# Zero-padded keys by head for the first dilation group's scores in an encoder trunk

## The chip, the cores and the metric

The kernel runs on one core of a Trainium2 chip. The metric is the device time of one execution in microseconds; lower is better. Engines are named as in the profile: PE is TensorE's matmuls, PEld its weight loads, DVE is VectorE, ACT is ScalarE, POOL is GpSimd, SP is the engine that issues the DMAs.

## The reference

A trunk of four residual layers over one sequence of 256 tokens and 1024 channels. Each layer has a token mixer and a SwiGLU channel mixer, each between two RMS norms. Layers 0 and 3 mix by retention, layer 1 by a convolution module, layer 2 by dilated attention. The change is in layer 2. There, 16 heads of 64 channels have three groups of queries, keys and values, one for each dilation (1, 4, 16); the outputs of the three groups are merged by their softmax denominators:

```python
def _dilated_attention_mixer(h, w_in, w_out):
    proj = (h @ w_in).reshape(B, S, N_ATTN_GROUPS, 3, ATTN_HEADS, ATTN_HEAD_DIM)
    ...
    for g, (window, dil) in enumerate(DILATION_GROUPS):   # (128, 1), (512, 4), (2048, 16)
        q = prope(proj[:, :, g, 0])
        k = prope(proj[:, :, g, 1])
        v = proj[:, :, g, 2]
        o, l = _dilated_band_attention(q, k, v, dil, window // (2 * dil))
        outs.append(o)
        lses.append(l)
    wts = jax.nn.softmax(jnp.stack(lses, 0), axis=0)
    o = jnp.sum(wts[..., None] * jnp.stack(outs, 0), axis=0).astype(h.dtype)
    return o.reshape(B, S, ATTN_HEADS * ATTN_HEAD_DIM) @ w_out
```

Merging by the denominators is the same as one softmax over the keys of all three groups side by side, and the kernel does it so.

## The kernel before

The tokens are two tiles of 128 (t = 0, 1), reordered so that tokens of the same residue modulo 4 lie together. Every float32 operand of a product is kept as two parts, a high part in the format that TensorE takes and the low rest; a product is then three matmuls (high x high, high x low, low x high). `split` (line 49) makes the parts: line 50 copies the high part on ScalarE, line 51 subtracts it from the source on VectorE. Weights come through `load_w` by DMA into one of seven raw buffers and are split in the same way into one of ten pairs of buffers `wh`, `wl`.

The attention layer (`attention`) loops over eight pairs of heads. For a pair it projects queries, keys and values (`roped` and `vproj`, both through `proj`, whose matmuls are line 181: 24 of 384 columns for one tile of tokens), turns queries and keys with identity matmuls (`flip3`, L693) into a PSUM bank with channels in the rows, and splits them. `kflip` (L706) does this for the keys: the bank holds 128 rows by three blocks of 128 columns. Block 0 holds the keys of dilation 1, head 0 in rows 0 to 63 and head 1 in rows 64 to 127; one split of 128x128 puts it into `kh`, `kl` (tags `akh`, `akl`). Blocks 1 and 2 hold, for head 0 and head 1, the two other dilations in the two halves of the rows; they go by two splits of 64x256 into `kbh`, `kbl`, whose other places were set to zero once, at lines 670 and 671.

`softmax(t, h, st)` (L724) makes the scores of one tile of queries and one head into one PSUM bank: the first 256 columns are dilation 1, three matmuls of line 729 that contract the 64 rows of head h; the last 256 columns are the two other dilations, three matmuls of line 731 that contract all 128 rows, where the zeros in `kbh`, `kbl` keep the dilations apart. Then VectorE adds the mask and takes the row's extreme (L736), ScalarE takes the exponential (L746), and VectorE normalises (L747, L748). For a pair it is called four times, (t, h) = (0,0), (0,1), (1,0), (1,1).

The probabilities are turned (`flip`, L757) and multiplied with the values (`values`, L772: 12 matmuls of 256 columns) inside the next pair's projections. So TensorE's order for a pair is: the scores of the pair before, query projection, two flips, key projection, and so on up to the value projection of tile 1, after which its own scores follow. The second `kflip` of a pair stands ahead of the value projection of tile 1 (inside it for the first pair). The framework lists the instructions of each engine by priority and readiness in a model of its own, so weight casts for the next pair stand between the small steps on ScalarE and VectorE, and the order on an engine is fixed when the kernel is built. Accesses to one PSUM bank are ordered among engines by semaphores.

Of the kernel before, what the change touches and what calls it, by code (L numbers as in the profile page):

```python
# [8 lines left out]
F32 = mybir.dt.float32  # L9
F32R = mybir.dt.float32r  # L10
# [4 lines left out]
P = 128  # L15
D = 1024
# [4 lines left out]
PAIRS = 8  # L21
# [16 lines left out]
def tile_trunk(ctx: ExitStack, tc: tile.TileContext, a):  # L38
    nc = tc.nc
# [9 lines left out]
    def split(h, l, src):  # L49
        ia = nc.scalar.copy(h, src)  # L50
        iv = nc.vector.tensor_sub(l, src, h.bitcast(F32))  # L51
        return ia, iv
# [23 lines left out]
        with tc.issue_after(cast[0].ins), tc.issue_after(cast[1].ins):  # L76
            yield

# [1 line left out]
    xs = [const.tile([P, D], F32, tag=f"x{t}", name=f"x{t}") for t in range(2)]  # L80
    grow = work.tile([1, D], F32, tag="gain", name="grow", bufs=2)
    nc.sync.dma_start(grow, a["norm_w"][0:1, :])
# [120 lines left out]
                    stop=(last and i == 2),  # L203
                )

# [1 line left out]
    def retention_decay(j, pool):  # L207
        tmp = pool
        dist = work.tile([P, 2, 512], F32, tag="fg", name="dist", bufs=1)
# [19 lines left out]
            dts.append(dt)  # L229
        return dts  # L230

# [1 line left out]
    def retention(j, gload, decay, finish, pool, first):  # L233
        dts = []
        rope = pool.tile([P, 2, 2, P], F32, tag="rope", name="rope", bufs=1)
# [276 lines left out]
    def conv(j, finish, pool, prefetch):  # L512
# [9 lines left out]
        cvp = pool.tile([P, KB, 256], F32, tag="cvp", name="cvp", bufs=1)  # L522

        def perm(v):
            # natural token 4 u + r, read as (r, u)
            return v.rearrange("p (u r) -> p r u", r=4)

        def glu(t, c, ws, mid=None):
# [80 lines left out]
        for t in range(2):  # L609
# [15 lines left out]
            h = const.tile([P, KB, P], F32R, tag=f"xTh{t}", name=f"yh{t}")  # L625
            l = const.tile([P, KB, P], F32R, tag=f"xTl{t}", name=f"yl{t}")
            for hh in range(2):
                tp = bank("aux")
# [34 lines left out]
    def attention(j, finish, pool):  # L663
# [5 lines left out]
        kbl = pool.tile([P, 2, 2, 256], F32R, tag="kbl", name="kbl", bufs=1)  # L669
        nc.vector.memset(kbh.bitcast(F32), 0.0)  # L670
        nc.vector.memset(kbl.bitcast(F32), 0.0)
        oh = pool.tile([P, PAIRS, 256], F32R, tag="oh", name="oh", bufs=1)
        ol = pool.tile([P, PAIRS, 256], F32R, tag="ol", name="ol", bufs=1)

# [21 lines left out]
        def ts_(t):  # L696
            return slice(t * P, (t + 1) * P)
# [7 lines left out]

        def kflip(t, st, r):  # L706
            tp = flip3(r)
            if t == 0:
                st["kh"] = pool.tile([P, 256], F32R, tag="akh", name="akh", bufs=1)
                st["kl"] = pool.tile([P, 256], F32R, tag="akl", name="akl", bufs=1)  # L710
            split(st["kh"][:, ts_(t)], st["kl"][:, ts_(t)], tp[:, 0:P])
            tv = tp[:, P : 3 * P].rearrange("p (h d) -> p h d", h=2)
            for rows, cols in ((slice(0, 64), slice(0, P)), (slice(64, P), slice(P, 256))):
                split(kbh[rows, :, t, cols], kbl[rows, :, t, cols], tv[rows])
# [7 lines left out]
            split_scaled(st["vh"][:, t, :], st["vl"][:, t, :], b[:, 0:384], rsx[t])  # L722

        def softmax(t, h, st):  # L724
            qh, ql, kh, kl = st["qh"], st["ql"], st["kh"], st["kl"]
            rows = slice(h * 64, h * 64 + 64)
            b = bank("acc")
            for n, (x, y) in enumerate(((qh, kh), (qh, kl), (ql, kh))):
                nc.tensor.matmul(b[:, 0:256], lhsT=x[rows, 0, ts_(t)], rhs=y[rows, :], start=(n == 0), stop=(n == 2))  # L729
            for n, (x, y) in enumerate(((qh, kbh), (qh, kbl), (ql, kbh))):  # L730
                nc.tensor.matmul(  # L731
                    b[:, 256:512], lhsT=x[:, 1 + h, ts_(t)], rhs=y[:, h, t, :], start=(n == 0), stop=(n == 2)
                )
            pe = pool.tile([P, 512], F32, tag="ape", name="ape", bufs=APE)
            sc = work.tile([P, 4], F32, tag="asc", name="asc", bufs=4)
            nc.vector.tensor_tensor_reduce(  # L736
                out=pe,
                in0=b,
                in1=mask[:, t, :],
                op0=ALU.add,  # L740
                op1=ALU.min,
                scale=-0.125,
                scalar=3e38,
                accum_out=sc[:, 0:1],
            )
            nc.scalar.activation(pe, pe, AF.Exp, scale=-1.0, bias=sc[:, 0:1], accum_out=sc[:, 1:2])  # L746
            nc.vector.reciprocal(sc[:, 2:3], sc[:, 1:2])  # L747
            nc.vector.tensor_scalar_mul(pe, pe, sc[:, 2:3])  # L748
            return pe
# [38 lines left out]
        for pr in range(PAIRS):  # L788
            st = {"wq": w3(pr, 0)}
# [53 lines left out]
        outp(1, range(4, KB))  # L843
        finish(1, acc[1])

# [1 line left out]
    pre_norm(0, gain0, late=True)  # L847

    for i in range(DEPTH):
# [3 lines left out]
        def finish(t, f):  # L853
            post_norm(t, f, gains[0])
            pre_norm(t, gains[1])
# [27 lines left out]
            ffn(i, finish_ffn, pool)  # L883


# [1 line left out]
def _layout(inputs):  # L887
    import numpy as np

    f32 = np.float32  # L890
    pos = np.arange(256)
    tok = 4 * (pos % 64) + pos // 64
    c = {}
    c["x"] = inputs["x"].reshape(256, D)[tok].reshape(2, P, D)
    c["ident"] = np.eye(P, dtype=f32)
    c["norm_w"] = inputs["norm_w"].reshape(4 * DEPTH, D)
    c["log1m"] = inputs["ret_log1m_decay"].reshape(-1, 8)
    c["ffn_w_in"] = (
        inputs["ffn_w_in"].reshape(DEPTH, 4, 2, P, 2, FFN_GROUPS, 256).transpose(0, 5, 1, 3, 2, 4, 6)
        .reshape(DEPTH, FFN_GROUPS, 4, P, 1024)  # L900
    )
    c["ffn_w_out"] = inputs["ffn_w_out"].reshape(DEPTH, 2 * FFN_GROUPS, P, D)
    w = inputs["ret_w_in"]
    nr = w.shape[0]
    qk = w[:, :, : 2 * D].reshape(nr, D, 2, RET_HEADS, 256).transpose(0, 3, 1, 2, 4).reshape(nr, RET_HEADS, 1, D, 512)
    vg = w[:, :, 2 * D :].reshape(nr, D, 2, RET_HEADS, 512).transpose(0, 3, 2, 1, 4)
    w = np.concatenate([qk, vg], axis=2)
    c["ret_w_in"] = (
        w.reshape(nr, RET_HEADS, 3, 4, 2, P, 512).transpose(0, 1, 2, 3, 5, 4, 6).reshape(nr, RET_HEADS, 3, 4, P, 1024)
    )  # L910
    c["ret_w_out"] = inputs["ret_w_out"].reshape(nr, 16, P, D)
    w = inputs["conv_w_in"]
    n = w.shape[0]
    c["conv_w_in"] = (
        w.reshape(n, 4, 2, P, 2, 4, 256).transpose(0, 5, 1, 3, 2, 4, 6).reshape(n, 4, 4, P, 1024)
    )
    c["conv_w_dw"] = inputs["conv_w_dw"].reshape(n, TAPS, KB, P).transpose(0, 3, 2, 1)
    chv = [inputs[k].reshape(n, 1, KB, P) for k in ("conv_b_dw", "conv_ln_g", "conv_ln_b")]
    chv.append(inputs["conv_b_in"].reshape(n, 2, KB, P))
    c["conv_ch"] = np.concatenate(chv, axis=1).transpose(0, 3, 1, 2)  # L920
    c["conv_w_out"] = inputs["conv_w_out"].reshape(n, KB, P, D)
    c["conv_b_out"] = inputs["conv_b_out"]
    w = inputs["attn_w_in"]
    n = w.shape[0]
    w = w.reshape(n, D, 3, 3, PAIRS, 2, 64)  # group, qkv, pair, head of pair, dim
    qk = w[:, :, :, 0:2].transpose(0, 4, 3, 1, 5, 2, 6)  # n pair qk D head group dim
    g0 = qk[:, :, :, :, :, 0].reshape(n, PAIRS, 2, D, 128)
    g12 = qk[:, :, :, :, :, 1:3].reshape(n, PAIRS, 2, D, 256)
    qk = np.concatenate([g0, g12], axis=4)
    v = w[:, :, :, 2].transpose(0, 3, 1, 2, 4, 5).reshape(n, PAIRS, 1, D, 384)  # L930
    w = np.concatenate([qk, v], axis=2)
    c["attn_w_in"] = (
        w.reshape(n, PAIRS, 3, 4, 2, P, 384).transpose(0, 1, 2, 3, 5, 4, 6).reshape(n, PAIRS, 3, 4, P, 768)
    )
    c["attn_w_out"] = inputs["attn_w_out"].reshape(n, KB, P, D)
    # tables of positions only
    tf = tok.astype(f32)
    diff = tok[None, :] - tok[:, None]  # query n minus key m, [m, n]
    dist = np.stack([np.maximum(diff, 0), np.maximum(-diff, 0)]).astype(f32)  # 2, m, n
    c["ret_dist"] = dist.reshape(2, 2, P, 256).transpose(2, 0, 1, 3).reshape(P, 2, 512)  # L940
    inv = (1.0 / (f32(10000.0) ** np.linspace(0.0, 1.0, 128, dtype=f32))).astype(f32)
    ang = tf[:, None] * inv[None, :]
    c["ret_rope"] = np.stack([np.cos(ang), np.sin(ang)], axis=1).reshape(2, P, 2, P).transpose(1, 0, 2, 3)
    inv = (f32(500000.0) ** (-np.arange(0, 16, 2, dtype=f32) / f32(16))).astype(f32)
    ang = tf[:, None] * inv[None, :]
    cs = np.stack([np.concatenate([np.cos(ang)] * 2, 1), np.concatenate([np.sin(ang)] * 2, 1)], axis=1)
    c["attn_rope"] = cs.reshape(2, P, 2, 16).transpose(1, 0, 2, 3)
    masks = []
    for t in range(2):
        rows = tok[t * P : (t + 1) * P]  # L950
        near = np.abs(rows[:, None] - tok[None, :]) <= 64
        c1 = (rows[:, None] - rows[None, :]) % 4 == 0
        c2 = (rows[:, None] - rows[None, :]) % 16 == 0
        masks.append(np.where(np.concatenate([near, c1, c2], axis=1), 0.0, -1e30))
    c["attn_mask"] = np.stack(masks, axis=1).astype(f32)
    return {k: np.ascontiguousarray(v, dtype=f32) for k, v in c.items()}, tok
# [22 lines left out]
```

## Time and profile before

| | |
|---|---|
| median of 3 runs | 1625.04 us (1624.56 to 1625.5) |
| span of the profiled execution | 1623.5 us |
| PE busy | 1604.0 us (99%) |
| PEld busy | 1345.9 us (83%) |
| DVE busy | 1038.4 us (64%) |
| ACT busy | 864.0 us (53%) |

The span runs from the first to the last instruction; the profile gives no other time for the profiled execution. The attention layer's matmuls begin at about 723 us and its last scores end at 1003 us. The bars of matmuls overlap, since they are pipelined: what one costs is read from start to start. In the timeline a row has its start and length in us, the engine, the line, the operation, the tiles written and read, and in brackets the idle time of that engine before it with what ended it. A row marked x2 or x3 merges instructions that follow on each other.

### The profile page before, as it was taken

The numbers are of one execution on the slowest core, as the hardware profiler recorded it, in microseconds if no ns is written. First come the engines' busy times: TensorE is split into PE (matmuls) and PEld (weight loads), VectorE is DVE, ScalarE is ACT, GpSimd is POOL, SyncE is SP. The second block draws the span as 40 slices with busy tenths as digits, with TensorE's granted clock in tenths as the row PEclk, the third lists the DMA queues.
The fourth block names the chain that finished last, engine by engine and source line by source line (L and its number), as shares of the span: only waits on it lengthen the run. The fifth ranks groups of instructions, "written<-read, shape, count | busy, mean of one in ns | idle before, by whom it ended". The sixth has DMA issues, their size and how long they took to land.

```text
span 1623.5 us, 20999 instructions
## 1 busy us (share of the span) xinstructions
PE 1604.0 (99%) x7742; PEld 1345.9 (83%) x7742; DVE 1038.4 (64%) x1576; ACT 864.0 (53%) x1376; POOL 69.8 (4%) x106
## 2 busy tenths in 40 slices
PE   9999999999999999999999999999999999999998
PEld 6888878888787788889999999788888888878886
DVE  7755685546797854557777767755567655675452
ACT  7544464445687644546656656644456444555341
POOL 1000010001000100010000000100010000010000
PEclk9999999999999999999999999999999999999999
DMA  8645474655304755544444444564655543475530
GB/s 316 234 137 178 156 244 171 203 185 182 121 1 145 254 200 179 169 131 142 153 147 131 143 143 156 202 213 168 205 174 169 180 167 127 160 238 194 194 117 26
DMA packets 79882, 274.27 MB, mean 169 GB/s; under 512 B 9378, under 2 KB 9634, under 8 KB 79779
## 3 DMA queue, kind: packets, MB, share of 16 engines
q1 hardware_dynamic: 79778, 272.92, 49.7%
q8 instruction: 61, 1.00, 0.2%
q14 instruction: 43, 0.34, 0.1%
HBM read 271.84 MB, written 1.05 MB: 168 GB/s over the span
## 4 chain that ended last, share of the span: by engine, by line
PE 91%; DVE 3%; ACT 2%; DMA 2%; issue 1%; POOL 0%; SPq 0%; DVEq 0%; POOLq 0%; ACTq 0%
PE mm L181 58%; PE acc L198 20%; PE acc L575 3%; PE aux L322 1%; PE acc L772 1%; PE aux L457 1%; DMA raw<-in_ffn_w_out 1%; PE acc L731 1%; PE acc L729 1%; PE aux L757 1%; DVE wl L51 1%; ACT junk L116 1%; PE aux L298 1%; DMA raw<-in_ffn_w_in 1%; PE aux L693 1%
## 5 line engine op out<-in xcount | busy, mean ns | idle before, releaser
L181 PE MATMUL mm<-wh,xTh 128*128 128x512 f32 (+1 forms) x1536 | 596.8, 389 | 0.8 <-ACT xTh L50 0.8
L181 PE MATMUL mm<-wh,xTl 128*128 128x512 f32 (+1 forms) x1536 | 583.1, 380 | 0.0
L181 PE MATMUL mm<-wl,xTh 128*128 128x512 f32 (+1 forms) x1536 | 582.6, 379 | 0.0
L51 DVE TENSOR_TENSOR wl<-raw,wh 128x1024 fp32r<-128x1024 f32 (+1 forms) x432 | 497.5, 1163 | 118.9 <-ACT wh L50 107.9
L50 ACT CAST wh<-raw 128x1024 fp32r<-128x1024 f32 (+1 forms) x432 | 429.1, 1003 | 141.7 <-PE mm L181 107.8
L181 PEld LDWEIGHTS mm<-wh,xTl 128*128 128x128 f32 x1536 | 289.1, 188 | 50.2 <-DVE xTl L51 0.3
L181 PEld LDWEIGHTS mm<-wl,xTh 128*128 128x128 f32 x1536 | 289.8, 189 | 44.5 <-DVE wl L51 0.5
L181 PEld LDWEIGHTS mm<-wh,xTh 128*128 128x128 f32 x1536 | 289.3, 188 | 44.8 <-ACT xTh L50 1.2
L446 ACT ACTIVATE fsg<-mm,rsx 128x256 f32<-128x256 f32 x88 | 41.7, 473 | 171.6 <-PE mm L181 171.6
L448 DVE SCALAR_TENSOR_TENSOR fsg<-mm,rsx,fsg 128x256 f32<-128x256 f32 x88 | 42.3, 481 | 127.7 <-ACT fsg L446 127.5
L51 DVE TENSOR_TENSOR pooll<-raw,poolh 128x1024 fp32r<-128x1024 f32 x88 | 107.4, 1222 | 9.2 <-ACT poolh L50 7.9
L198 PE MATMUL acc<-poolh,fhh 128*128 128x512 f32 x344 | 108.6, 396 | 0.5 <-ACT fhh L50 0.5
L198 PE MATMUL acc<-poolh,fhl 128*128 128x512 f32 x344 | 107.3, 392 | 0.0
L198 PE MATMUL acc<-pooll,fhh 128*128 128x512 f32 x344 | 107.1, 393 | 0.0
L50 ACT CAST poolh<-raw 128x1024 fp32r<-128x1024 f32 x88 | 92.2, 1049 | 26.7 <-PE acc L198 15.4
L51 DVE TENSOR_TENSOR fhl<-aux,fhh 128x256 fp32r<-128x256 f32 x88 | 37.0, 421 | 98.4 <-ACT fhh L50 98.4
L50 ACT CAST fhh<-aux 128x256 fp32r<-128x256 f32 x88 | 32.5, 369 | 115.6 <-PE aux L457 115.6
L198 PEld LDWEIGHTS acc<-pooll,fhh 128*128 128x128 f32 x344 | 64.6, 188 | 14.5
L198 PEld LDWEIGHTS acc<-poolh,fhh 128*128 128x128 f32 x344 | 63.7, 188 | 15.4 <-ACT fhh L50 2.7
L198 PEld LDWEIGHTS acc<-poolh,fhl 128*128 128x128 f32 x344 | 64.3, 188 | 14.6
L559 DVE SCALAR_TENSOR_TENSOR cv<-upad,wdw,cv 128x256 f32<-128x256 f32 x143 | 59.5, 479 | 0.8
L108 POOL TENSOR_SCALAR rs<-ss 128x1 f32<-128x1 f32 x16 | 7.5, 468 | 1061.5 <-ACT junk L116 1061.5
(178 smaller groups left out, 1617.2 us busy)
## 6 DMA issues: line engine op xcount, KB each, us to landing
raw<-in_ffn_w_in SPq DMA_DIRECT2D x176, 512.0 KB, 4.8
raw<-in_ret_w_in SPq DMA_DIRECT2D x96, 512.0 KB, 4.6
raw<-in_ffn_w_out SPq DMA_DIRECT2D x88, 512.0 KB, 4.4
raw<-in_attn_w_in SPq DMA_DIRECT2D x96, 384.0 KB, 3.7
raw<-in_ret_w_out SPq DMA_DIRECT2D x32, 512.0 KB, 4.7
raw<-in_conv_w_in SPq DMA_DIRECT2D x16, 512.0 KB, 4.6
gain<-in_norm_w SPq DMA_DIRECT2D x15, 512.0 KB, 5.2
raw<-in_conv_w_out SPq DMA_DIRECT2D x8, 512.0 KB, 4.0
```

Of the source, the lines that this page charges most:

```text
L50: ia = nc.scalar.copy(h, src)
L51: iv = nc.vector.tensor_sub(l, src, h.bitcast(F32))
L116: nc.scalar.activation(junk, src, AF.Square, scale=scale, accum_out=acc)
L181: nc.tensor.matmul(out, lhsT=st[t][:, k, :], rhs=mv[:, sl], start=(n == 0), stop=(n == 23))
L198: nc.tensor.matmul(acc[hh], lhsT=st, rhs=mv[:, hh * 512 : hh * 512 + 512], start=(first and i == 0), stop=(last and i == 2),)
L298: nc.tensor.matmul(b[:, m * 256 : (m + 1) * 256], lhsT=kt[:, 2 + half, m * P : (m + 1) * P], rhs=qt[:, half, :], start=(n == 0), stop=(n = ...
L322: nc.tensor.matmul(b, lhsT=pt[:, m, t * P : (t + 1) * P], rhs=vt[:, m, :], start=(n == 0), stop=(n == 5))
L446: nc.scalar.activation(sg, b[:, 0:256], AF.Silu, scale=rsx[t])
L448: nc.vector.scalar_tensor_tensor(out=sm, in0=b[:, 256:512], scalar=rsx[t], in1=sg, op0=ALU.mult, op1=ALU.mult)
L457: nc.tensor.transpose(tp[:, k * P : (k + 1) * P], sm[:, k * P : (k + 1) * P], ident)
L559: last_tap["v"] = nc.vector.scalar_tensor_tensor(out=cv, in0=upad[:, cb, w : w + 256], scalar=wdw[:, cb, w : w + 1], in1=cv, op0=ALU.mult, ...
L575: nc.tensor.matmul(pc[:, 0:256], lhsT=dgs[w], rhs=upad[:, cb, w : w + 256], start=(w == 0), stop=(w == TAPS - 1),)
```

## The change

The keys of dilation 1 no longer lie in `kh`, `kl` with both heads in the rows. There are two tiles `kah`, `kal` of 128 rows, two heads and 256 keys, set to zero once at the start of the layer. `kflip` writes head 0's keys into rows 0 to 63 of place 0, head 1's into rows 64 to 127 of place 1, by two splits of 64x128 in place of one of 128x128. The three matmuls of line 729 take all 128 rows of the queries and of the head's place; the other head's queries meet zeros. The tiles `akh`, `akl`, which were allocated anew for each pair (one buffer), are gone; nothing else differs but comments.

```diff
         nc.vector.memset(kbh.bitcast(F32), 0.0)
         nc.vector.memset(kbl.bitcast(F32), 0.0)
+        kah = pool.tile([P, 2, 256], F32R, tag="kah", name="kah", bufs=1)
+        kal = pool.tile([P, 2, 256], F32R, tag="kal", name="kal", bufs=1)
+        nc.vector.memset(kah.bitcast(F32), 0.0)
+        nc.vector.memset(kal.bitcast(F32), 0.0)
...
         def kflip(t, st, r):
             tp = flip3(r)
-            if t == 0:
-                st["kh"] = pool.tile([P, 256], F32R, tag="akh", name="akh", bufs=1)
-                st["kl"] = pool.tile([P, 256], F32R, tag="akl", name="akl", bufs=1)
-            split(st["kh"][:, ts_(t)], st["kl"][:, ts_(t)], tp[:, 0:P])
+            for h, rows in ((0, slice(0, 64)), (1, slice(64, P))):
+                split(kah[rows, h, ts_(t)], kal[rows, h, ts_(t)], tp[rows, 0:P])
...
         def softmax(t, h, st):
-            qh, ql, kh, kl = st["qh"], st["ql"], st["kh"], st["kl"]
-            rows = slice(h * 64, h * 64 + 64)
+            qh, ql = st["qh"], st["ql"]
             b = bank("acc")
-            for n, (x, y) in enumerate(((qh, kh), (qh, kl), (ql, kh))):
-                nc.tensor.matmul(b[:, 0:256], lhsT=x[rows, 0, ts_(t)], rhs=y[rows, :], start=(n == 0), stop=(n == 2))
+            for n, (x, y) in enumerate(((qh, kah), (qh, kal), (ql, kah))):
+                nc.tensor.matmul(b[:, 0:256], lhsT=x[:, 0, ts_(t)], rhs=y[:, h, :], start=(n == 0), stop=(n == 2))
```

## Rows read from the trace of the kernel before

**Rows 1.** The page's busy table: busy us, share of the span, instructions.
```profile
PE 1604.0 (99%) x7742; PEld 1345.9 (83%) x7742; DVE 1038.4 (64%) x1576; ACT 864.0 (53%) x1376; POOL 69.8 (4%) x106
```
**Rows 2.** Windows view: one pair, scores to scores; busy us (instructions), clock, DMA.
```profile
785.89:821.36 35.47, 35.47 (x222) 34.10 (x221) 25.68 (x64) 21.26 (x43) 0.00 (x0) 1.00 0.42 134
```
**Rows 3.** Timeline of TensorE: the second pair's scores, their entry and their end.
```profile
785.45 0.34 PE L181 MATMUL mm<-wl,xTh 128*128 128x384 f32 x1
785.62 0.34 PE L181 MATMUL mm<-wh,xTl 128*128 128x384 f32 x1
785.89 0.38 PE L729 MATMUL acc<-akh,aqh 64*128 64x256 f32 x1
786.12 0.28 PE L729 MATMUL acc<-akl,aqh 64*128 64x256 f32 x1
786.23 0.28 PE L729 MATMUL acc<-akh,aql 64*128 64x256 f32 x1
786.44 0.38 PE L731 MATMUL acc<-kbh,aqh 128*128 128x256 f32 x1
...
790.18 0.34 PE L181 MATMUL mm<-wh,xTh 128*128 128x384 f32 x1
```
**Rows 4.** Timeline of TensorE: 12 value products, 12 retention scores, first and follower.
```profile
1017.26 0.28 PE L772 MATMUL acc<-pth,avh 128*128 128x256 f32 x1
...
1018.70 0.63 PE L198 MATMUL acc<-wh,oh 128*128 128x512 f32 x2
...
1391.87 0.28 PE L298 MATMUL aux<-qkh 128*128 128x256 f32 x1
...
1393.31 0.39 PE L181 MATMUL mm<-wh,xTh 128*128 128x512 f32 x1
```
**Rows 5.** Tile views: count, ns min/median/max of small splits, first and last start, forms.
```profile
L51 DVE TENSOR_TENSOR akl<-aux,akh x16: 281/282/284, 742.0 to 995.5; 128x128 fp32r<-128x128 f32 x16
...
L50 ACT CAST oh<-acc x32: 258/259/262, 766.0 to 1022.9; 64x128 fp32r<-64x128 f32 x32
...
L51 DVE TENSOR_TENSOR ol<-acc,oh x32: 273/284/296, 766.3 to 1023.7; 64x128 fp32r<-64x128 f32 x32
```
**Rows 6.** Timeline of VectorE and ScalarE: end of a first tile's kflip.
```profile
808.87 0.41 DVE L51 TENSOR_TENSOR kbl<-aux,kbh 64x256 fp32r<-64x256 f32 x1
...
809.71 0.43 DVE L51 TENSOR_TENSOR kbl<-aux,kbh 64x256 fp32r<-64x256 f32 x1 [0.24 <-ACT kbh L50]
...
809.31 0.37 ACT L50 CAST kbh<-aux 64x256 fp32r<-64x256 f32 x1 [0.81 <-DVE kbl L51]
```
**Rows 7.** Timeline of VectorE and ScalarE: a second tile's kflip up to the reductions.
```profile
782.65 0.28 DVE L51 TENSOR_TENSOR akl<-aux,akh 128x128 fp32r<-128x128 f32 x1
...
784.62 0.41 DVE L51 TENSOR_TENSOR kbl<-aux,kbh 64x256 fp32r<-64x256 f32 x1
784.95 1.88 DVE L51 TENSOR_TENSOR wl<-raw,wh 128x768 fp32r<-128x768 f32 x2
786.86 0.43 DVE L51 TENSOR_TENSOR kbl<-aux,kbh 64x256 fp32r<-64x256 f32 x1
...
787.86 0.68 DVE L736 CUSTOM_DVE_ANT_0 ape<-acc,mask 128x512 f32<-128x512 f32 x1
...
788.46 0.69 DVE L736 CUSTOM_DVE_ANT_0 ape<-acc,mask 128x512 f32<-128x512 f32 x1
...
785.00 0.84 ACT L50 CAST wh<-raw 128x768 fp32r<-128x768 f32 x1 [0.25 <-PE mm L181]
```
**Rows 8.** Timeline of VectorE and TensorE: the layer's start.
```profile
726.94 0.91 DVE L671 MEMSET kbl<- 128x1024 f32 x1 [0.16 <-issue]
727.77 1.22 DVE L139 TENSOR_TENSOR xg<-x,gain 128x512 f32<-128x512 f32 x2
...
730.77 0.49 PE L160 MATMUL aux<-ident,xg 128*128 128x128 f32 x3
```
**Rows 9.** Timeline of TensorE: the first value products after the last pair.
```profile
1009.56 0.27 PE L757 MATMUL aux<-ident,ape 128*128 128x128 f32 x1
```

## Prediction, made before the changed kernel was run

> **What bounds the kernel now.** I read the page's busy table first. TensorE is busy 1604.0 us of 1623.5 [rows 1], so a change pays only if it shortens TensorE's own stream, and it costs only if it makes TensorE wait. The span is 1623.5 us and the three timed runs lie at 1624.56 to 1625.5 us with a median of 1625.04, so about 1.5 us lie outside the span; the sums below are made in the span and taken off the median.
>
> Then the stage: the attention layer runs eight head pairs, and the windows view of one pair [rows 2] shows 35.47 us with TensorE busy all of it, VectorE 25.68 and ScalarE 21.26. Nothing but TensorE is late there; VectorE has 9.8 us to spare in a pair, ScalarE 14.2.
>
> Last, TensorE's timeline of one pair's scores [rows 3]: 24 matmuls of 256 columns, four groups (two token tiles, two heads) of three with 64 contracted rows (L729) and three with 128 (L731). The reader is to look at starts, not at the lengths of the bars, since bars overlap. Inside a triple the third matmul starts 0.11 us after the second (786.12 to 786.23). But from the first to the second it is 0.23 us (785.89 to 786.12), and from the last of one triple to the first of the next 0.21 us (786.23 to 786.44). So each change of row count costs about 0.2 us over two matmul slots, and there are eight changes in a pair. The whole block takes 785.89 to 790.18, 4.29 us, and its entry from the projection takes 0.27 us (785.62 to 785.89) where that stream steps by 0.17 (785.45 to 785.62). The timeline shows no wait on another engine inside the block.
>
> **The matmuls, L728 to L733.** The count of matmuls and of columns stays; only the contracted rows of the 96 L729 matmuls of the layer's 192 score matmuls go from 64 to 128. What 256-column, 128-row matmuls cost in an unbroken stream is in two places: the value products of L772 between two output products, 12 in 1.44 us (1017.26 to 1018.70), and the retention scores of L298, 12 in 1.44 us (1391.87 to 1393.31) [rows 4]. That is 0.120 us each, entry and exit included. The new block is 24 x 0.120 = 2.88 us. Saved: 4.29 - 2.88 = 1.41, and 0.27 - 0.17 = 0.10 at the entry, so 1.51 us a pair and 8 x 1.51 = 12.1 us in all. Cross-check: the first slot of a triple and the step into it are 0.23 + 0.21 where 2 x 0.12 would do, 0.20 too much, by eight 1.6.
>
> [...]
>
> **The key split, kflip, L711.** One split of 128x128 (a ScalarE copy, then a VectorE subtraction that reads it) becomes two of 64x128, 16 times. On VectorE akl takes 0.282 us and a 64x128 piece of the same kind, ol, 0.284 [rows 5]: half the rows save nothing. So VectorE gets 16 x 0.28 = 4.5 us more, ScalarE by the row of oh (0.259 a piece) 16 x 0.26 = 4.1 us. Per pair that is 0.57 and 0.52 us against 9.8 and 14.2 spare: hidden as work. If that cover were gone, the price would be those 4 to 5 us.
>
> What matters more is the latency of the chain. All pieces of one kflip read one PSUM bank, and the copy of a piece on ScalarE waits for the subtraction before it: kbh at 809.31 sat idle 0.81 us until kbl had ended [rows 6]. So the change adds one step (copy, handover, subtraction) to a serial chain, and the last piece, the second kbl of the second token tile, comes later. Queued behind it on VectorE are the value split and the softmax reductions (L736); the matmul of the fourth group that reads it waits too.
>
> - When it is ready now: the chain's VectorE steps start at 782.65, 784.62 and 786.86 [rows 7]; the last ends at 787.29.
> - When it will be needed: the new block starts at 785.62 + 0.17 = 785.79; the fourth group's first 128-row matmul is number 22, at 785.79 + 21 x 0.12 = 788.31, and the one that reads kbl at 788.43. The cover is 1.14 us.
> - What a step adds: the trace does not show a kflip with four steps, so I bound it by the distances between steps that it shows. In the first tile's kflip 0.84 us (808.87 to 809.71) [rows 6], in the second's 1.97 and 2.24 [rows 7]. The long ones are long because weight casts of 0.94 us lie between: at 784.95 two of them go ahead of the last kbl. At 0.84 the wait is nothing; at 2.24 it is 1.10 us a pair, 8.8 us in all. I take 1.2 us, between them and nearer the short end: the last casts wait for the weight buffers that the value projection gives back (0.25 us of idle before the cast at 785.00, ended by L181, [rows 7]), and that projection ends where the block starts, so a later step has fewer casts to fall behind. That is a wait of 0.06 us a pair, 0.5 us in all.
>
> A gain beyond the sum from this part is excluded: nothing is taken out of the chain.
>
> **The memsets.** Two of 128x512 once, at the layer's start. The present ones of 128x1024 take 0.91 us [rows 8], so I estimate 0.46 each. VectorE is then on the way to the second tile's transposes: xg ends at 728.99, the transposes start at 730.77. The 1.8 us between hide 0.9 us; without that cover the cost is 0.9 us once. In the other tiles nothing moves: no DMA, no queue, and the weights of a pair are the same bytes in 1.5 us less of 35.47, 4% more per us.
>
> **The sum.** 12.1 saved, less 0.5 for the chain and about 0.4 for what shifts at the edges (half of the memsets' price) = 11.2 us. 1625.04 - 11.2 = 1613.8 us.
>
> **Rivals.**
>
> 1. *The chain is late.* The added step falls among weight casts and takes 1.4 to 2.24 us, so that TensorE waits 0.3 to 1.1 us in the fourth group of each pair. For it: both steps in the second tile's kflip are that long. Against it: the order on TensorE is not the program's alone; at 1009.56 one transpose of L757 sits among the value products of L772 [rows 9], so a late operand can be covered by the next projection. Time: 12.1 - 2.1 to 12.1 - 8.8 saved, 1615 to 1622 us.
> 2. *The steps cost the same as before.* If the extra 0.2 us came with a new accumulation group, or with the change between the halves of a bank, and not with the row count, the stream would keep its holes: 1625 plus up to 1 us for the memsets, no change. Against it: the retention scores put two groups into the halves of one bank, and the value products change banks on the way in and out, both without a hole [rows 4]. [...]
> 3. *Slower.* One mechanism: the last kbl is put behind softmax reductions on VectorE. The step adds 2.24 us, and three reductions at 0.60 us (787.86 to 788.46, [rows 7]) go ahead: it then ends at 787.29 + 2.24 + 1.80 = 791.33, and TensorE waits 2.90 us a pair where it gained 1.51: 8 x 1.39 = 11.1 us more, 1636 us. It decides from 2.65 us of delay on (1.14 of cover and 1.51 of gain). Against it: the subtraction has its place in the program ahead of the reductions, and it is so in the trace, where kbl at 786.86 comes before the first reduction at 787.86.
>
> **How the numbers follow.** The forecast, 1611.5 to 1615 us, has 0.68: its centre is 1613.8, its low end the full 12.1 plus the few tenths by which 0.120 may be too much, its high end 10 us saved. Rival 1 has 0.21, of which a quarter (0.05) lies above 1620. Rival 2 has 0.03, rival 3 0.04. The remaining 0.04 are a gain above 13.5 us. A range from 1611.5 to 1619 leaves out 0.04 below, 0.07 of rival 1 and 0.07 of rivals 2 and 3, together 0.18. Faster by over 0.2% (3.25 us, about what a measurement of this kernel can tell from no change) takes the forecast, the gain above it and rival 1 but for its last 0.02: 0.91. The same: rival 2 and that rest, 0.05. Slower: 0.04.
>
> **What would show it.** In the profile after: the scores of a pair in 2.8 to 2.95 us with starts 0.12 apart and no longer first matmul in a triple; the pair at about 34.0 us in place of 35.47; kah and kal as 32 pieces of 64x128 each at 0.26 and 0.28 us. The chain's step is right if the last kbl ends before the fourth group needs it. A hole of some tenths ahead of the fourth group's 128-row matmuls would show rival 1, a hole ahead of every first matmul rival 2, reductions ahead of the last kbl rival 3. I am wrong if the 0.2 us stay although all rows are 128, or if TensorE's waits in the layer grow by more than 2 us.

## The result, and the profile after

The changed kernel takes 1615.42 us (median of five, 1614.31 to 1615.72) beside 1625.04 us for the kernel before: ratio 0.9941, interval 0.9928 to 0.9953, 9.6 us less. The forecast was 1613.8 us, 11.2 less, in a range of 1611.5 to 1619. The span went from 1623.5 to 1614.0 us.

The page's busy table of the changed kernel, and the windows view of one pair (busy us and instructions of PE, PEld, DVE, ACT, POOL, then granted clock, DMA share, GB/s):

```profile
PE 1593.4 (99%) x7742; PEld 1343.2 (83%) x7742; DVE 1046.8 (65%) x1594; ACT 870.9 (54%) x1392; POOL 69.9 (4%) x106
...
784.61:818.81 34.20, 34.20 (x222) 33.83 (x221) 26.64 (x65) 22.11 (x45) 0.00 (x0) 1.00 0.46 139
```

TensorE lost 10.6 us of busy time [rows 1]; a pair takes 34.20 us where it took 35.47 [rows 2], with the same count of instructions on it. VectorE gained 8.4 us, ScalarE 6.9, both hidden. The same pair's scores in TensorE's timeline:

```profile
784.61 0.34 PE L181 MATMUL mm<-wh,xTl 128*128 128x384 f32 x1
784.79 0.28 PE L731 MATMUL acc<-kah,aqh 128*128 128x256 f32 x1
...
785.02 0.28 PE L731 MATMUL acc<-kah,aql 128*128 128x256 f32 x1
785.14 0.28 PE L733 MATMUL acc<-kbh,aqh 128*128 128x256 f32 x1
...
786.58 0.28 PE L733 MATMUL acc<-kbh,aqh 128*128 128x256 f32 x1
786.83 0.39 PE L733 MATMUL acc<-kbl,aqh 128*128 128x256 f32 x1
787.06 0.28 PE L733 MATMUL acc<-kbh,aql 128*128 128x256 f32 x1
787.17 0.28 PE L731 MATMUL acc<-kah,aqh 128*128 128x256 f32 x1
...
787.89 0.34 PE L181 MATMUL mm<-wh,xTh 128*128 128x384 f32 x1
```

Against [rows 3], the eight holes of a pair are gone: the entry takes the projection's own step (784.61 to 784.79), and starts are 0.12 us apart within a triple and from one triple to the next (L731 to L733). One hole is new. In the third group the matmul that reads kbl starts 0.25 us after its neighbour (786.58 to 786.83), and the next 0.23 later. So the block takes 3.10 us in place of the 2.88 that were forecast. The weight load at 786.83 names what it waited for, and VectorE's timeline shows the chain behind it:

```profile
786.83 0.19 PEld L733 LDWEIGHTS acc<-kbl,aqh 128*128 128x128 f32 x1 [0.18 <-DVE kbl L51]
...
781.64 0.27 DVE L51 TENSOR_TENSOR kal<-aux,kah 64x128 fp32r<-64x128 f32 x1
782.73 0.96 DVE L51 TENSOR_TENSOR wl<-raw,wh 128x768 fp32r<-128x768 f32 x1 [0.81 <-ACT wh L50]
783.72 0.29 DVE L51 TENSOR_TENSOR kal<-aux,kah 64x128 fp32r<-64x128 f32 x1
784.05 0.96 DVE L51 TENSOR_TENSOR wl<-raw,wh 128x768 fp32r<-128x768 f32 x1
785.04 0.42 DVE L51 TENSOR_TENSOR kbl<-aux,kbh 64x256 fp32r<-64x256 f32 x1
785.38 0.94 DVE L51 TENSOR_TENSOR wl<-raw,wh 128x768 fp32r<-128x768 f32 x1
786.35 0.43 DVE L51 TENSOR_TENSOR kbl<-aux,kbh 64x256 fp32r<-64x256 f32 x1
```

The last kbl ends at 786.78, 2.17 us after the last matmul of the projection started (784.61). In the kernel before it was 787.29 - 785.62 = 1.67 us [rows 3, 7]. The chain is longer by 0.50 us.

The whole effect can be laid out by landmarks in TensorE's timeline of each kernel's profile: the first projection matmul of the attention layer, the last projection matmul ahead of a pair's scores, and the first matmul of the FFN that follows. All in us; the last column goes by a span given to 0.1 us:

| kernel | start to scores 1 | scores 1 to 2 | scores 2 to 8 | scores 8 to FFN | sum | after the FFN's start |
|---|---|---|---|---|---|---|
| before | 30.90 | 35.46 | 212.80 | 32.17 | 311.33 | 592.91 |
| changed | 31.06 | 34.22 | 205.19 | 31.36 | 301.83 | 592.84 |
| e1_rows64 | 31.06 | 34.77 | 212.80 | 31.47 | 310.10 | 591.93 |
| e2_one_split | 30.85 | 33.96 | 203.76 | 30.62 | 299.19 | 591.92 |
| e3_copies_first | 31.08 | 34.07 | 203.76 | 31.79 | 300.70 | 591.79 |
| e4_heads_alternate | 30.87 | 33.63 | 201.76 | 31.60 | 297.86 | 592.11 |
| e5_by_head | 30.89 | 33.63 | 201.80 | 31.58 | 297.90 | 592.87 |
| e7_rows_alternate | 30.89 | 42.77 | 251.52 | 38.30 | 363.47 | 592.88 |

The changed kernel saves 311.33 - 301.83 = 9.50 us in this layer and nothing behind it. What stands ahead of the layer moves by up to 2 us between profiles (it starts at 718.2 to 720.2), so the layer's own sum is a better measure of a step than the time of the whole.

### The profile page after: what moved, and what is told of

Read it like the earlier page. It is cut to its first block, busy times and chain, and to the rows that moved or that the text cites. A ratio compares the mean times of both kernels' runs of the same rounds, so it can differ in the third digit from the quotient of the medians.

```text
span 1614.0 us, 21034 instructions
## 1 busy us (share of the span) xinstructions
PE 1593.4 (99%) x7742; PEld 1343.2 (83%) x7742; DVE 1046.8 (65%) x1594; ACT 870.9 (54%) x1392; POOL 69.9 (4%) x106
## 4 chain that ended last, share of the span: by engine, by line
PE 92%; DVE 2%; ACT 2%; DMA 1%; issue 1%; POOL 0%; SPq 0%; DVEq 0%; POOLq 0%; ACTq 0%
PE mm L181 59%; PE acc L198 21%; PE acc L575 3%; PE aux L322 1%; PE acc L774 1%; PE aux L457 1%; PE aux L759 1%; DMA raw<-in_ffn_w_out 1%; PE acc L733 1%; PE aux L298 1%; PE aux L160 1%; ACT junk L116 1%; PE acc L731 1%; PE aux L698 1%; DVE wl L51 1%
```

## The experiments

The theory: each change between 64 and 128 contracted rows costs TensorE 0.19 us (1.51 us of a pair over its eight changes); the change takes all eight out of a pair, 12.1 us in all, and the longer chain of key pieces gives 2.6 back. The rivals: the holes belong to something else (groups, halves of a bank), or the 2.6 us went elsewhere.

**e1_rows64: the new key tiles and splits, the old row count.**

```diff
-                nc.tensor.matmul(b[:, 0:256], lhsT=x[:, 0, ts_(t)], rhs=y[:, h, :], start=(n == 0), stop=(n == 2))
+                nc.tensor.matmul(b[:, 0:256], lhsT=x[rows, 0, ts_(t)], rhs=y[rows, h, :], start=(n == 0), stop=(n == 2))
```

> The keys are stored as in the changed kernel (kah, kal by head, two splits of 64x128), but the score matmuls of the first dilation group contract only the 64 rows of their head. Theory (each change between 64 and 128 contracted rows costs about 0.19 us on TensorE, and the split's extra step only hurts where the shorter score block asks for its result sooner): the block stays at 4.29 us, the extra step is covered, time 1624.8 to 1626 us. Rival (the holes come with accumulation groups or halves of a bank, the gain of the change from somewhere else, such as the order of the small steps): about 1615 us as the changed kernel.

Measured: 1624.08 us beside 1625.33 for the kernel before on the same chip, ratio 0.9994 (0.9985 to 1.0003): no change that the interval can tell, and 0.7 us below the range that was written. TensorE's timeline of the same block, and a row of the last pair:

```profile
786.00 0.34 PE L181 MATMUL mm<-wh,xTl 128*128 128x384 f32 x1
786.27 0.38 PE L732 MATMUL acc<-kah,aqh 64*128 64x256 f32 x1
786.49 0.28 PE L732 MATMUL acc<-kal,aqh 64*128 64x256 f32 x1
786.61 0.28 PE L732 MATMUL acc<-kah,aql 64*128 64x256 f32 x1
786.82 0.38 PE L734 MATMUL acc<-kbh,aqh 128*128 128x256 f32 x1
...
1001.26 0.39 PE L732 MATMUL acc<-kah,aqh 64*128 64x256 f32 x2
```

The old holes are all back (0.27 at the entry, 0.22, 0.21) and the block is 4.28 us. So the gain is the row count, and the split's extra pieces cost nothing while the block is long: 212.80 us for the six middle pairs, to the hundredth as before. The layer as a whole is 1.23 us shorter, by 0.7 us in the first pair and 0.7 in the last. There TensorE's order differs from before: the 64-row triples of two heads stand together, and matmuls start in twos (x2 at 1001.26, the next two 0.22 us later, then 0.12), which e4 and e5 below make use of.

**e2_one_split: the new row count, the old split.**

```diff
-                nc.tensor.matmul(b[:, 0:256], lhsT=x[rows, 0, ts_(t)], rhs=y[rows, :], start=(n == 0), stop=(n == 2))
+                nc.tensor.matmul(b[:, 0:256], lhsT=x[:, 0, ts_(t)], rhs=y, start=(n == 0), stop=(n == 2))
```

> The kernel before with one edit: the score matmuls of the first dilation group contract all 128 rows of the unpadded keys, so both heads' products are summed (the separation of the heads is left out); the key split stays one of 128x128. Theory (the whole gain is 12.1 us on TensorE, and the changed kernel loses 2.7 us of it to the longer chain of key pieces): block of 2.88 us without a wait, 1612.6 to 1613.6 us. Rival (the missing 2.7 us lie elsewhere, as in weights that come too late for a faster TensorE): 1615 us as the changed kernel.

Measured: 1612.43 us, ratio 0.9922 (0.9908 to 0.9935), 0.2 us below the range that was written. From TensorE's timeline, the entry, the place where the changed kernel waits (third group), and the end:

```profile
784.90 0.34 PE L181 MATMUL mm<-wh,xTl 128*128 128x384 f32 x1
785.07 0.28 PE L729 MATMUL acc<-akh,aqh 128*128 128x256 f32 x1
...
786.99 0.28 PE L731 MATMUL acc<-kbl,aqh 128*128 128x256 f32 x1
787.11 0.28 PE L731 MATMUL acc<-kbh,aql 128*128 128x256 f32 x1
...
787.95 0.34 PE L181 MATMUL mm<-wh,xTh 128*128 128x384 f32 x1
```

24 matmuls in 2.88 us without a hole, a pair in 33.96 us, the layer in 299.19: 12.14 us less than before. The term of the forecast for TensorE was 12.1. The 2.64 us that the changed kernel lacks against this one are therefore what the padding costs: 0.21 up to the first scores, 0.26 in the first pair, 1.43 in the six middle ones (0.24 each), 0.74 in the last.

**e3_copies_first: the changed kernel with the chain taken apart.**

```diff
-            for h, rows in ((0, slice(0, 64)), (1, slice(64, P))):
-                split(kah[rows, h, ts_(t)], kal[rows, h, ts_(t)], tp[rows, 0:P])
...
-                split(kbh[rows, :, t, cols], kbl[rows, :, t, cols], tv[rows])
+            for hi, lo, src in parts:
+                nc.scalar.copy(hi, src)
+            for hi, lo, src in parts:
+                nc.vector.tensor_sub(lo, src, hi.bitcast(F32))
```

> The changed kernel, with the four copies of a key flip issued on ScalarE first and the four subtractions on VectorE after them, so that the chain has one handover in place of seven; the pieces and the matmuls are the same. Theory (the 2.7 us are the chain of alternating pieces in one PSUM bank): the last kbl ends before the third score group of the pair needs it, 1612.8 to 1613.8 us. Rival (the delay is the weight casts that lie between, or the number of pieces, whatever their order): 1615 us.

Measured: 1613.6 us, ratio 0.9932 (0.992 to 0.9945). ScalarE's and VectorE's timelines of the same flip:

```profile
780.42 0.53 ACT L720 CAST kah<-aux 64x128 fp32r<-64x128 f32 x2
780.98 0.75 ACT L720 CAST kbh<-aux 64x256 fp32r<-64x256 f32 x2
...
781.75 0.61 DVE L722 TENSOR_TENSOR kal<-aux,kah 64x128 fp32r<-64x128 f32 x2 [0.58 <-ACT kbh L720]
782.39 0.86 DVE L722 TENSOR_TENSOR kbl<-aux,kbh 64x256 fp32r<-64x256 f32 x2
```

Four copies, one handover, four subtractions: the last kbl ends at 783.25, before the scores begin (784.06 is the last projection matmul), and no weight cast lies between. The six middle pairs take 203.76 us, the same as e2: this part of the loss was the chain, and the order of the pieces alone removes it. The run does not part the handovers from the weight casts that slip in between them: both go. The end of the layer does not follow: 31.79 us against 30.62. There, the first output matmul waits for a reduction:

```profile
990.75 0.28 PE L738 MATMUL acc<-kbh,aql 128*128 128x256 f32 x1
991.85 0.50 PE L198 MATMUL acc<-wh,oh 128*128 128x512 f32 x1 [0.82 <-DVE asc L743]
...
987.05 3.50 DVE L51 TENSOR_TENSOR wl<-raw,wh 128x1024 fp32r<-128x1024 f32 x3
...
991.11 0.68 DVE L743 CUSTOM_DVE_ANT_0 ape<-acc,mask 128x512 f32<-128x512 f32 x1
```

The scores hold all four `acc` banks, and the output product needs one back; the first reduction stands behind three casts of 3.5 us on VectorE. That is read from this trace, not tried apart.

**after_again and e3_again: both on one chip.**

> The changed kernel itself, to stand beside the next run on the same chip: 1615.4 us within 0.7, third score group of a pair 0.22 us late behind the second kbl.

> The changed kernel with the four copies of a key flip first and the four subtractions behind them, beside the changed kernel on the same chip. If the chain of alternating pieces costs the 2 us, it is 1.5 to 2.3 us faster than the changed kernel here too (blocks of 2.88 us in place of 3.10 in pairs 2 to 7); if the earlier difference was between runs, both agree within 0.7 us.

Measured: 1616.27 us for the changed kernel (ratio 0.994, 0.9927 to 0.9952), 0.9 us above what was expected and so just outside the 0.7, and 1614.68 for copies first (0.9934, 0.9921 to 0.9948). The difference of 1.6 us has the forecast size, but the intervals overlap, so the times alone do not settle it. The landmarks repeat: 205.17 and 203.76 us for the six middle pairs, 301.85 and 300.64 for the layer, so 1.2 us in the layer.

**e7_rows_alternate: a change at every matmul.** The order is 64 rows, 128 rows, 64 rows, each product into another head's bank than its neighbour:

```diff
+                    for n in range(3):
+                        x, y = one[n]
+                        nc.tensor.matmul(
+                            bs[t, h][:, 0:256], lhsT=x[rows, 0, ts_(t)], rhs=y[rows, :], start=(n == 0), stop=(n == 2)
+                        )
+                        x, y = two[n]
+                        nc.tensor.matmul(
+                            bs[t, 1 - h][:, 256:512],
...
```

> The kernel before with the same 24 matmuls of a pair in an order that changes the row count at each one (64, 128, 64, ..., each product into another bank than its neighbour): 24 changes in place of 8. If each change costs 0.19 us: 8 x 16 x 0.19 = 24 us more, about 1649 us. If a change costs only where it follows a run of equal ones, or the holes came with the groups: within 5 us of the kernel before.

Measured: 1676.24 us, ratio 1.0311 (1.0297 to 1.0325): 51 us slower, twice what was expected. TensorE's timeline, then the windows view (columns as above):

```profile
793.84 0.38 PE L734 MATMUL acc<-akh,aqh 64*128 64x256 f32 x1
794.15 0.38 PE L738 MATMUL acc<-kbh,aqh 128*128 128x256 f32 x1
...
800.10 0.58 PE L734 MATMUL acc<-akh,aqh 64*128 64x256 f32 x1
800.60 0.58 PE L738 MATMUL acc<-kbh,aqh 128*128 128x256 f32 x1
...
793.84:797.00 3.16, 3.16 (x12) 1.88 (x11) 1.98 (x3) 1.64 (x3) 0.00 (x0) 1.00 0.81 264
800.00:803.00 3.00, 3.00 (x7) 1.79 (x7) 0.00 (x0) 0.00 (x0) 0.00 (x0) 0.50 0.02 5
806.00:809.00 3.00, 3.00 (x21) 2.96 (x20) 0.39 (x2) 0.49 (x2) 0.00 (x0) 1.00 0.36 125
```

At a granted clock of 1.00 the starts are 0.313 us apart, 0.19 more than the 0.120 of an unbroken stream: the price of one change, as assumed. Then the granted clock falls to 0.50 (800 to 803) and the steps become 0.51 us; it is back at 1.00 in the projection behind (806 to 809). The steps lengthen so in each of the eight blocks, after 9 to 18 of them, and the mean granted clock of the execution is 0.977 beside 0.997 before. From scores to scores a pair takes 42.0 us in the mean of seven, 6.6 more than before: 24 x 0.313 - 4.28 = 3.2 are the changes, and the remaining 3.3 are put down to the clock, an estimate by difference. The theory's term holds; that the granted clock would fall in this block was not expected, and what lowers it was not tried apart.

**e4_heads_alternate and e5_by_head: 64 rows kept, fewer changes.** Both take the kernel before and put the twelve 64-row matmuls of a pair ahead of the twelve others:

```diff
+            for t, n, h in [(t, n, h) for t in range(2) for n in range(3) for h in range(2)]:   # e4
+            for t, n, h in [(t, n, h) for t in range(2) for h in range(2) for n in range(3)]:   # e5
+                x, y = one[n]
+                rows = slice(h * 64, h * 64 + 64)
+                nc.tensor.matmul(
+                    bs[t, h][:, 0:256], lhsT=x[rows, 0, ts_(t)], rhs=y[rows, :], start=(n == 0), stop=(n == 2)
+                )
```

> The kernel before with another order of the 24 score matmuls of a pair: first the twelve of 64 rows, the two heads (rows 0 to 63 and rows 64 to 127) alternating, then the twelve of 128 rows; two changes of row count in place of eight. Theory A (only the change between 64 and 128 rows costs, 0.19 us each): 8 x 6 x 0.19 = 9.0 us saved, about 1616 us. [...] Theory C (a change of the rows' half costs as much as a change of the count): fourteen changes, 8 x 6 x 0.19 = 9 us lost, about 1634 us.

> The kernel before with the twelve 64-row matmuls of a pair first, head by head in groups of three (no two heads alternating inside a group), then the twelve of 128 rows: two changes of row count a pair, as with alternating heads, but only at three places do different halves of the rows meet. If alternating heads ran side by side, this one loses most of that: block of 24 x 0.12 + 0.19 plus 0.10 at the entry, at most 3 x 0.12 less; 1616 us, down to 1613 if each meeting saves a slot. If the order alone and not the overlap made the alternating kernel fast: 1611.4 us.

Measured: 1611.43 us (0.9915, 0.9901 to 0.9928) and 1611.12 us (0.9912, 0.9898 to 0.9925). TensorE's timeline of e4, then of e5:

```profile
784.03 0.34 PE L181 MATMUL mm<-wh,xTl 128*128 128x384 f32 x1
784.29 0.39 PE L731 MATMUL acc<-akh,aqh 64*128 64x256 f32 x2
784.52 0.28 PE L731 MATMUL acc<-akl,aqh 64*128 64x256 f32 x2
...
785.20 0.39 PE L736 MATMUL acc<-kbh,aqh 128*128 128x256 f32 x1
...
786.74 0.34 PE L181 MATMUL mm<-wh,xTh 128*128 128x384 f32 x1
```

```profile
783.02 0.39 PE L731 MATMUL acc<-akh,aqh 64*128 64x256 f32 x2
783.25 0.29 PE L731 MATMUL acc<-akl,aqh 64*128 64x256 f32 x2
783.36 0.28 PE L731 MATMUL acc<-akh,aql 64*128 64x256 f32 x2
...
785.47 0.34 PE L181 MATMUL mm<-wh,xTh 128*128 128x384 f32 x1
```

Two heads' matmuls of the same kind (x2) share one step (0.23 us for the first, 0.11 or 0.12 for the next, where one matmul alone took as much): the twelve take six steps. e4 lies 4.6 us below the 1616 that theory A wrote for the changes alone, and far from the 1634 of theory C. The block is 2.45 us with its two changes of row count: 4.29 less six changes at 0.19 and six shared steps at 0.12 makes 2.43. Of e5 the forecast failed: its program gives three matmuls of head 0 and then three of head 1, yet the starts come in twos, and it is as fast as e4. The time is the one that had been written for "the order alone and not the overlap", but the trace does not bear that reading out: 24 matmuls at 0.12 us one after the other would make 2.88, and the block is 2.45 (783.02 to 785.47). Starting in twos does not need alternating order here: with runs of three the starts are 0.23, then 0.11 or 0.12 us apart, as in e4. Both layers take 297.9 us, and on one chip e5 stands 5 us ahead of the changed kernel (after_again) with intervals that do not meet: the faster version keeps the 64 rows.

## Why the prediction was right, and where it was not

- **TensorE's term was right.** 12.1 us forecast, 12.14 in e2, where it stands alone; a pair 33.96 us where 35.47 - 1.51 was worked out. The step of 0.120 from [rows 4] held. The low end of the range allowed for a shorter step; no run showed one for full rows: e2's 24 matmuls take 2.88 us.
- **The hole belongs to the row count.** The rival that the steps cost the same is out by e1 (holes back with 64 rows, same tiles) and by e7 (0.19 us for each change). What TensorE does in that time no trace shows; the price alone is read.
- **The chain of key pieces was right in kind and mis-sized twice.** The cover of 1.14 us was the wrong step: it took the last kbl to be needed by the fourth group alone. But the two pieces of kbh and kbl are the two halves of the rows, and both hold both heads, so the third group's matmuls already contract over both. Its kbl matmul is number 17, due at 785.79 + 16 x 0.12 = 787.71, and the cover was 787.71 - 787.29 = 0.42 us. The added step, taken at 1.2 us from bounds of 0.84 to 2.24, was 0.50, below both bounds, because the casts fell otherwise: before, two lay in the second gap of the chain [rows 7] and one, at 783.74, in the first, and now one lies in each of three gaps (782.73, 784.05, 785.38). The true cover less the true step leaves 0.08 us of lateness beside the 0.06 of the forecast. That the two nearly agree is luck: the cover and the step were each put 0.7 us too high. And lateness is not what the wait costs: it cost 0.24 us a pair, since the stream steps twice by more than 0.12 (0.25 and 0.23 us). Eight pairs at 0.06 were forecast, 0.5 us; six pairs lost 1.43, all eight 2.43, and in the middle pairs the loss fell in the third group and not the fourth. So the time lies inside the wide range but 0.4 us outside the forecast proper (1611.5 to 1615 us), at the low end of rival 1, which named this mechanism with 0.3 to 1.1 us a pair. Start to start, TensorE lost more than the 2 us that the prediction had set as a sign of being wrong.
- **The edges** were put at 0.4 us. Up to the first scores 0.21 is missing, in the last pair 0.74. There the chain is slower, since the casts of the output weights are longer (128x1024, 1.22 us beside 0.95 for 128x768), and TensorE waits for kbh itself: 0.38 us idle at 992.66, a start 0.54 us later than the step of 0.12 would have it. The memsets took 0.485 us each (0.46 had been estimated) and the second tile's transposes started at 730.81 in place of 730.77 [rows 8]: covered.

```profile
992.00 0.28 PE L731 MATMUL acc<-kah,aql 128*128 128x256 f32 x1
992.66 0.50 PE L733 MATMUL acc<-kbh,aqh 128*128 128x256 f32 x2 [0.38 <-ACT kbh L50]
...
L51 DVE TENSOR_TENSOR kal<-aux,kah x32: 272/285/297, 742.1 to 989.4; 64x128 fp32r<-64x128 f32 x32
...
L675 DVE MEMSET kah<- x1: 485/485/485, 729.1 to 729.1; 128x512 f32 x1
```

- **The pieces' own work** was right: a 64x128 subtraction takes 0.285 us where one of 128x128 took 0.282 [rows 5], so half the rows save nothing, and it is hidden in VectorE's idle time. The page's busy time rose by more than the 4.5 and 4.1 us of the forecast and the memsets (8.4 and 6.9); it counts bars that overlap once, so it moves with their order too, and the rest was not taken apart.
- **Slower** did not come: the subtractions stayed ahead of the reductions in the middle pairs (786.35 against 787.35). In the last pair one reduction did go ahead of the last kbl (991.85 against 992.64), but only once.

Open: the end of the layer. In the changed kernel 0.54 of the last pair's 0.74 us stand at the late kbh. With kbh early, e3 waits there for a bank instead, so that the 0.74 were not won back; e4 and e5 too are about 1 us slower at the end than e2 (31.6 against 30.62). It was not taken further.

## What to carry to other kernels

When TensorE is the bound, read start to start: here the holes that returned in each block at the changes of row count were a cost of the sequence. Half-filled rows cost nothing in themselves (64-row matmuls step by 0.11 us inside a triple [rows 3], full ones by 0.120), only the change to full rows and back, 0.19 us each. Before padding small contractions with zeros, try putting the small ones together: those on different halves of the rows started here in twos, a step of 0.12 us for both (e4, e5), and that beat the padding by 4 to 5 us without any extra pieces (in the layer, 297.86 us against 301.83, and against 300.70 for the padded kernel with its copies first). When a stream gets shorter, look up for each operand which is the first matmul to need it, by the slices it reads, and if small evacuations of one bank go back and forth between two engines, try issuing all of one engine's first (e3: 203.76 us in place of 205.19 for the six middle pairs).

## What the runs showed of the hardware that was not expected

- Two runs of 64-row matmuls on different halves of the rows overlap even when the program lists one run whole before the other (e5: two starts every 0.12 us, block 2.45 us as with alternating order).
- With a change of row count at each of 24 matmuls, steps of 0.313 us with weight loads busy for 1.88 of 3.16 us, the granted clock fell from 1.00 to 0.50 within a block of some 9 us (793.84 to 803.02) and was back at 1.00 by 806 in the projection behind it: by the difference above about 3.3 us a pair on top of the 3.2 us of the changes themselves (e7). In the kernel before, with eight changes in blocks of 4.29 us, the granted clock was 1.00 over the whole pair [rows 2].
